# A one-core encoder block: sum reads and held squares in the gates, paced splits and other tile homes in the first MLP product, weight sums and pre-sums on other engines in the second

## The chip, the cores and the metric

The kernel runs on one core of a Trainium2 chip. The time is the device time of one execution in microseconds (us), given as the median of several runs; lower is better. The core has five engines that run side by side, each through its own list of instructions in order, and wait for each other by semaphores: TensorE (PE in the profile; its weight loads are PEld), VectorE (DVE), ScalarE (ACT), GpSimd (POOL) and SyncE (SP), which here issues the transfers (DMA).

## The reference, cut to what matters

One layer of an encoder with 1024 tokens of width 1024, all in float32:

```python
u = rms_norm(x, norm1_g)
q, k, v, cb, cc, ch, ga, gb = split(u @ w_in)
y_a = neighbourhood_attention(rms_norm(q), rms_norm(k), v, rpb) @ w_attn_branch
y_b = short_gated_conv(cb, cc, ch, conv_w) @ w_conv_branch
x = x + (sigmoid(ga) * y_a + sigmoid(gb) * y_b) @ w_o
x = x + square(relu(rms_norm(x, norm2_g) @ w_mlp_in)) @ w_mlp_out      # 1024 -> 4096 -> 1024
```

The change touches three stages: the gates (`ga`, `gb` with the products of the branches), the first MLP product (`w_mlp_in`) and the second (`w_mlp_out`).

## The kernel before, in words

**Arithmetic.** Every float32 operand is scaled by a power of two and split into two float16 halves, a head (the rounded value, made by ScalarE) and a rest (what is left, made by VectorE as scale x value - head). A product is three passes of matmuls: head x head, head x rest, rest x head. The scale comes from a bound on the operand: a sum of squares (ScalarE), added over the partitions by a matmul with ones, and turned into a power of two by five tiny VectorE instructions. Gates and both MLP products use seven products of half-size blocks in place of eight (sums and differences of blocks of weights and activations ahead, sums of products after); in the chunks 6 to 13 of the first MLP product one of the seven is cut in seven once more ("deep").

**Order of the work.** It is written out by hand. `unit` (L207) issues one group of usually 12 matmuls of 512 columns, then one turn of each hook, then the `post` of the unit before it (the VectorE or ScalarE instructions that read its PSUM bank), and then some turns of the two lists of generators: `step` for the foreground list `fg` (what must follow a product: relu, square, sums, store) and `tick` for the background list `bg` (what prepares weights to come). A turn of `bg` advances its first generator only; if that one answers `WAIT` and `side` is set, the next one gets the turn. So the two last arguments of `unit` set how early, in each engine's list, the preparation is issued. `apart` (L182) makes a generator wait until a number of units, or of matmul columns (`work`), has been issued. `need` and `built` run the background until an operand is complete. PSUM has eight banks, in three tags, taken in a fixed rota.

**Scale of an operand.** `scale_of` (L1152) waits for n units after the column of sums is ready, issues the matmul with ones (`all_sum`, L200), lets one more unit pass (`lag=1`), and only then issues VectorE's read of the result (L204) and the power of two (L435 to L442). `parts` (L1187) then issues heads (L1197) and rests (L1193) of three or four pieces, one turn each, a rest one turn after its head.

**Gates** (eight blocks n): seven units for the gates and four for the branches per block. While block n runs, `prep_s(n+1)` (L1211) scales the rows, sums blocks of weights on GpSimd (L1182), and makes the operand `w_s`. `norms1` (L1285) are three hooks that load each of 28 pieces of the first MLP weights into spare room and square them on ScalarE (L1296), a load and four units later a square; they are started after the gate units of block 2.

**First MLP product** (16 chunks q). `main1` (L1524) makes the operand of chunk q: GpSimd sums blocks (L1520), ScalarE and VectorE split, into the tile with tag V (even q) or B (odd q), not before chunk q-2 has been issued. `quad` (L1803) runs a whole chunk for q = 0 to 5, 14 and 15 (`whole`), with 2 background turns a unit for 2 < q < 14 and 5 otherwise; `pair` runs the deep chunks 6 to 13, whose extra operand `w_d` lies in the tile with tag K. After each chunk `h_done` (L1775) does relu (L1780) and square (L1782) on ScalarE, the block sums on GpSimd (L1408, VectorE for q = 0 and 1), and stores the result (L1794) to DRAM. SP takes all transfers in the order in which they are issued.

**Second MLP product** (four chunks s of seven pairs o; pair n = 7s + o). `prep2` (L1984) squares the weights (L1999, L2002), sums them, makes the pre-summed block T2 on GpSimd (L2008, L2009), and then for each pair loads the stored activation (`h_load`, L1980), splits it (L2034, L2036) and the weights (L2039, L2045) into a tile `ops` whose home rotates over the tags K, V and B, and updates blocks of weights for later pairs by GpSimd sums (L2050, L2054, L2058). Each pair is four units of 12 matmuls; their posts add into `acc` (L2135) or into the output `x` (L2144). In the last chunk `combine` (L2101) adds the accumulators into the output, partly on VectorE (L2108, L2112, L2115), partly on GpSimd (L2106, L2110, L2114), and each block of the output is stored as it is complete.

## Time and profile before

| | |
|---|---|
| median of 3 runs (range) | 1205.78 us (1203.58 to 1205.84) |
| the profiled execution: time, span | 1205.79 us, 1204.0 us |
| granted TensorE clock | 0.999 |
| gates / output product / first MLP product / second, by the trace | from about 298 / 530 / 614 / 904 us to 1199 us |

The span is the time from the first to the last instruction of the trace; the profiled execution took 1.8 us more than its span. Rows of the view of waits read: engine, the tile written and its line, the engine, tile and line waited for, and then the microseconds in total, how often, and the longest. Rows in order of time read: start, duration, engine, line, operation, tile written <- tiles read, shape, number of instructions merged, and in brackets the idle time before and what ended it. Rows of groups read: line, engine, operation, tiles, shape, count | busy us, mean ns of one | idle before. L12 is line 12 of the kernel; SPq is SP's queue of transfers. A matmul's end is modelled, so a matmul is drawn past the start of the next one.

### The profile page before, as it was taken

What the parts mean: (1) busy time and instruction counts of PE and PEld (TensorE: products, weight loads), DVE (VectorE), ACT (ScalarE), POOL (GpSimd) and SP (SyncE); (2) the same over time, 40 slices, a digit from 0 to 9 for tenths busy, and PEclk for the clock granted to TensorE, in tenths of its full rate; (3) what the DMA queues carried; (4) which work ended last, traced back from release to release, by engine and by line L of the source; (5) the groups of instructions that cost most, each with busy time, mean ns of one, the idle gap of its engine ahead of it and who ended that gap; (6) DMA issues with size and microseconds to landing.
All of it is one profiled execution on the core that took longest, in us unless ns stands there. A gap on an engine that the chain in (4) does not pass through costs nothing.

```text
span 1204.0 us, 16986 instructions
## 1 busy us (share of the span) xinstructions
PE 1186.2 (99%) x6265; PEld 579.7 (48%) x6265; DVE 975.0 (81%) x1654; ACT 754.7 (63%) x1175; POOL 455.3 (38%) x292
## 2 busy tenths in 40 slices
PE   8999999999999999999999999999998999999998
PEld 6444445555444444444477445555443444444443
DVE  6799888897468687878877767777559899999997
ACT  7866578776655767537766576667576743636440
POOL 2630011223221212001021567787677471554562
PEclk9999999999999999999999999999999999999999
DMA  9949456676544454442474445445465926335302
GB/s 289 216 160 206 109 127 137 115 147 135 114 114 139 159 183 149 140 166 114 97 165 143 156 158 192 176 142 181 158 236 201 369 80 226 121 138 194 105 35 105
DMA packets 181283, 189.61 MB, mean 157 GB/s; under 512 B 138192, under 2 KB 138704, under 8 KB 177104
## 3 DMA queue, kind: packets, MB, share of 16 engines
q1 hardware_dynamic: 181200, 188.52, 51.9%
q8 instruction: 49, 0.80, 0.3%
q14 instruction: 34, 0.28, 0.1%
HBM read 117.19 MB, written 37.75 MB: 129 GB/s over the span
## 4 chain that ended last, share of the span: by engine, by line
PE 61%; DVE 23%; ACT 8%; issue 5%; DMA 2%; SPq 0%; DVEq 0%; POOL 0%; ACTq 0%
PE ps_s L210 19%; PE ps_d L210 18%; PE ps_o L210 13%; PE ps_d L1069 8%; DVE ops L2045 2%; DVE ops L2036 2%; DVE w_s L1193 2%; PE ps_s L989 1%; PE ps_o L1046 1%; DVE w L1193 1%; DVE s L507 1%; ACT as L1782 1%; DMA w2x<-in_weights 1%; DVE sg L1342 1%; DVE w_ws L300 1%
## 5 line engine op out<-in xcount | busy, mean ns | idle before, releaser
L210 PEld LDWEIGHTS <-ops 128*128 128x128 f16 x1356 | 132.3, 98 | 162.0 <-issue 5.2
L210 PEld LDWEIGHTS <-w 128*128 128x128 f16 x1272 | 124.3, 98 | 129.3 <-DVE w L1193 1.6
L1069 PE MATMUL ps_d<-uT,w_ws 128*128 128x512 f16 x528 | 123.7, 379 | 0.0
L1408 POOL TENSOR_TENSOR as<-as 128x512 f32<-128x512 f32 x56 | 104.1, 1858 | 47.4 <-ACT as L1782 44.1
L210 PE MATMUL ps_d<-ops 128*128 128x512 f16 x516 | 118.4, 379 | 0.7 <-DVE ops L2045 0.7
L210 PE MATMUL ps_s<-ops 128*128 128x512 f16 x492 | 113.2, 379 | 2.6 <-DVE ops L2045 2.6
L2034 ACT ACTIVATE ops<-hf,sc 128x2048 f16<-128x2048 f32 x26 | 52.0, 2000 | 90.3 <-PE ps_s L210 47.1
L210 PEld LDWEIGHTS <-w_s 128*128 128x128 f16 x588 | 56.7, 98 | 70.6 <-DVE w_s L1193 2.9
L1520 POOL TENSOR_TENSOR tsum<-raw 128x512 f32<-128x512 f32 x28 | 39.4, 1417 | 126.9 <-ACT raw L1511 126.9
L210 PEld LDWEIGHTS <-uT 128*128 128x128 f16 x528 | 51.4, 98 | 62.1 <-issue 0.2
L210 PE MATMUL ps_o<-ops 128*128 128x512 f16 (+1 forms) x348 | 77.1, 372 | 0.7 <-DVE x L2144 0.7
L1069 PEld LDWEIGHTS <-w_ws 128*128 128x128 f16 x528 | 51.3, 98 | 54.1
L2036 DVE SCALAR_TENSOR_TENSOR ops<-hf,sc,ops 128x2048 f16<-128x2048 f32 x26 | 74.0, 2847 | 2.3 <-ACT ops L2034 2.2
L1182 POOL TENSOR_TENSOR gsum<-raw 128x512 f32<-128x512 f32 x14 | 19.1, 1377 | 134.5 <-ACT raw L1168 115.0
L210 PE MATMUL ps_d<-u2T,w 128*128 128x512 f16 (+1 forms) x288 | 60.9, 361 | 0.9 <-DVE as L1824 0.9
L1193 DVE SCALAR_TENSOR_TENSOR w<-raw,sc,w 128x1024 f16<-128x1024 f32 (+1 forms) x20 | 24.2, 1220 | 44.0 <-ACT w L1197 44.0
L1780 ACT ACTIVATE as<-as 128x2048 f32<-128x2048 f32 (+1 forms) x18 | 30.9, 1718 | 42.3 <-DVE as L1857 25.7
L1193 DVE SCALAR_TENSOR_TENSOR w<-tsum,sc,w 128x1024 f16<-128x1024 f32 x28 | 50.7, 1834 | 5.1 <-ACT w L1197 5.1
L210 PE MATMUL ps_s<-u2T,w 128*128 128x512 f16 (+1 forms) x252 | 52.7, 359 | 0.0
L1012 ACT ACTIVATE sz<-sz,sc 128x384 f32<-128x384 f32 (+1 forms) x64 | 37.2, 582 | 23.9 <-DVE sc L1003 16.6
L309 ACT ACTIVATE w_ws<-raw,sc 128x512 f16<-128x512 f32 (+2 forms) x72 | 40.6, 637 | 17.8 <-DVE sc L282 17.8
L210 PE MATMUL ps_s<-u2x,w 128*128 128x512 f16 (+1 forms) x228 | 49.8, 368 | 0.0
(419 smaller groups left out, 2720.0 us busy)
## 6 DMA issues: line engine op xcount, KB each, us to landing
raw<-in_weights SPq DMA_DIRECT2D x97, 512.0 KB, 4.5
hs<-as SPq DMA_DIRECT2D x16, 1792.0 KB, 7.9
hf<-hs SPq DMA_DIRECT2D x26, 1024.0 KB, 6.3
w2x<-in_weights SPq DMA_DIRECT2D x16, 512.0 KB, 7.4
raw<-in_weights SPq DMA_DIRECT2D x16, 384.0 KB, 3.5
mL<-in_weights SPq DMA_DIRECT2D x10, 512.0 KB, 4.5
mH<-in_weights SPq DMA_DIRECT2D x9, 512.0 KB, 4.3
xt<-in_x SPq DMA_DIRECT2D x8, 512.0 KB, 8.2
```

What stands on the lines that cost most here:

```text
L210: T.matmul(ps, l, r, start=a, stop=b, skip_group_check=free)
L309: A.activation(self.parts[:, 0, f + o:f + o + m], self.raw[p][:, o:o + m], AF.Copy, scale=sc[:, c:c + 1])
L1012: A.activation(z, z, AF.Exp, scale=-1.0, bias=sc[:, d["mx"]], accum_out=sc[:, d["sm"]])
L1069: T.matmul(ps, l, r, start=a, stop=b)
L1182: G.tensor_tensor(t[:, o], a, b, op=OP.add)
L1193: V.scalar_tensor_tensor(o(1), w, sc[:, s], o(0), op0=OP.mult, op1=OP.subtract)
L1408: sub.tensor_tensor(z[o], z[a], z[b], op=op)
L1520: G.tensor_tensor(t[:, o], a, b, op=OP.add)
L1780: A.activation(v[:, 0:4], v[:, 0:4], AF.Relu)
L2034: A.activation(P[:, 1, 0], hf, AF.Copy, scale=sc[:, Rs])
L2036: V.scalar_tensor_tensor(P[:, 1, 1], hf, sc[:, Rs], P[:, 1, 0], op0=OP.mult, op1=OP.subtract)
L2045: V.scalar_tensor_tensor(P[:, 0, 1, sl], w[i2], sc[:, fw], P[:, 0, 0, sl], op0=OP.mult, op1=OP.subtract)
```

## The change

- Gates: `prep_s` reads the sum at the first turn after its matmul (`lag` 0 in place of 1). From there until the operand is split, the hooks get no turns (`hold`). The hooks start after the gate units of block 1 in place of 2.
- First MLP product: for chunks 4 and 5 the rests are issued at most one per unit (`pace`). Chunks 3 to 5 give 4 background turns a unit in place of 2. The operand of chunk 15 may be made once chunk 12 has been issued (before: chunk 13), and goes into the tile with tag V; chunk 14's goes into the one with tag K. The homes of the `ops` tiles are shifted by one accordingly (pair 0 in B, 1 in K, 2 in V, and so on).
- Second MLP product: for s = 0 the scale waits three units in place of four. The weight sums after w11 and t2 are VectorE's (L2050, L2054); the one after t3 stays on GpSimd.
- Last chunk: the pre-sums of the accumulators (a6 with a1, a7 with a6) pass from VectorE to GpSimd, and are made one product earlier: a1 is added into a6 before the last product of a6 is added there, and a6 into a7 likewise.

```diff
@@ -176,7 +176,7 @@
-    late, units, forced, side, hooks = [], [0], [False], [False], []
+    late, units, forced, side, hooks, hold = [], [0], [False], [False], [], [False]
     work = [0]
@@ -209,7 +209,7 @@
         for g in list(hooks):
-            if not advance(g):
+            if not hold[0] and not advance(g):
                 hooks.remove(g)
@@ -1149,12 +1149,12 @@
-    def scale_of(am, more, n=3):
+    def scale_of(am, more, n=3, lag=1):
...
         b, s, inv = cols_of("prep", 1), cols_of("prep", 1), keep()
-        yield from all_sum(a, b, anybank(), 1e-36)
+        yield from all_sum(a, b, anybank(), 1e-36, lag)
         yield from pow2_half(b, 14, s, inv, more)
@@ -1184,12 +1184,17 @@
-    def parts(todo, s, then):
+    last_low = [-9]
+
+    def parts(todo, s, then, pace=False):
...
                 o, w = prev
+                if pace:
+                    yield from apart(last_low[0], 1)
+                    last_low[0] = units[0]
                 V.scalar_tensor_tensor(o(1), w, sc[:, s], o(0), op0=OP.mult, op1=OP.subtract)
@@ -1214,12 +1219,14 @@
         yield from forms_sum(ch, t, 2)
-        s, ch.inv = yield from scale_of(ch.sum, 9, 2)
+        s, ch.inv = yield from scale_of(ch.sum, 9, 2, 0)
+        hold[0] = True
         while done[0] < ch.first:
...
         ch.split = True
+        hold[0] = False
@@ -1328,7 +1335,7 @@
             sg = gate_units(n)
-            if n == 2:
+            if n == 1:
                 rooms = [v[:, 6:8].rearrange("p a t -> p (a t)").bitcast(F32) for v in M]
@@ -1343,6 +1350,7 @@
             branch_units(n, post)
+            assert n < 6 or not hooks
             late.append(lambda n=n, mf=mf: fg.append(m_done(n, mf)))
@@ -1464,7 +1472,7 @@
     pe_done, ready = [-2], set()
-    TAGS = ((base2, "B"), (base, "K"), (base, "V"))
+    TAGS = {i: ((base2, "B"), (base, "K"), (base, "V"))[(i - 16) % 3] for i in range(16, 44)}
     tsum = {}
@@ -1527,12 +1535,13 @@
             yield from sums_main(q)
-        while pe_done[0] < q - 1:
+        while (pe_done[0] < 1 if q == 2 else pe_done[0] < min(q - 1, 13)) or q == 14 and sub_done[0] < 12:
             yield
         m = int(deep)
-        pool, tag = ((base, "V"), (base2, "B"))[q % 2]
+        pool, tag = {14: (base, "K"), 15: (base, "V")}.get(q) or ((base, "V"), (base2, "B"))[q % 2]
         P = pool.tile([128, 7 - m, 2, 512], F16, name="w16_1", tag=tag)
         P1[q] = lambda w, i, k: P[:, w - m, i, k * 128:k * 128 + 128]
+        pace = q in (4, 5)
         todo = [] if deep else [(0, 1, ch.r[0][:, 0:1])]
@@ -1541,7 +1550,7 @@
         yield from parts([((lambda i, a=a, b=b: P[:, a - m:b - m, i]), w) for a, b, w in todo],
-                         at(s1, q // 2 - 1), then)
+                         at(s1, q // 2 - 1), then, pace)
         ready.add(q)
@@ -1557,7 +1566,7 @@
                           ((0, 2, x[:, 0].rearrange("p (h c) -> p h c", h=2)), (2, 3, y[:, 0:1, 256:]), (3, 7, d))],
-                         at(s1, q // 2 - 1), lambda n: None)
+                         at(s1, q // 2 - 1), lambda n: None, False)
         ready.add((0, q))
@@ -1835,7 +1844,7 @@
             2: lambda ps: V.tensor_tensor(z[0], ps[2], z[4], op=OP.add),
-            7: post7, 3: post3}, 2 if c1 == 512 else 3, 2 if 2 < q < 14 else 5, (1, 2, 5, 4, 6, 7, 3) if c0 else (1, 6, 5, 4, 2, 7, 3))
+            7: post7, 3: post3}, 2 if c1 == 512 else 3, 4 if 2 < q < 14 else 5, (1, 2, 5, 4, 6, 7, 3) if c0 else (1, 6, 5, 4, 2, 7, 3))
@@ -1991,7 +2000,7 @@
             yield from gate(16)
-            OPS[16] = TAGS[16 % 3][0].tile([128, 2, 2, 2048], F16, name="ops", tag=TAGS[16 % 3][1])
+            OPS[16] = TAGS[16][0].tile([128, 2, 2, 2048], F16, name="ops", tag=TAGS[16][1])
             j = OPS[16][:, 0, 0].bitcast(BF16)
@@ -2010,10 +2019,10 @@
             yield from gate(17)
-            P = OPS[17] = TAGS[17 % 3][0].tile([128, 2, 2, 2048], F16, name="ops", tag=TAGS[17 % 3][1])
+            P = OPS[17] = TAGS[17][0].tile([128, 2, 2, 2048], F16, name="ops", tag=TAGS[17][1])
             later["h", 1] = P[:, 0].rearrange("p w m -> p (w m)").bitcast(F32).rearrange("p (k t) -> p k t", k=4)
             SP.dma_start(later["h", 1], HS[0][:, ORDER[1][0]])
-        sw, inv = yield from scale_of(sums, 0, 4)
+        sw, inv = yield from scale_of(sums, 0, 3 + (s > 0))
         fw = keep()
@@ -2022,7 +2031,7 @@
             yield from gate(i)
-            pool, tag = TAGS[i % 3]
+            pool, tag = TAGS[i]
             if n > 1:
@@ -2047,11 +2056,11 @@
                 for i2 in range(2):
-                    G.tensor_tensor(w11[i2], w11[i2], w12[i2], op=OP.add)
+                    V.tensor_tensor(w11[i2], w11[i2], w12[i2], op=OP.add)
                 yield
...
                 for i2 in range(2):
-                    G.tensor_tensor(w12[i2], w12[i2], w22[i2], op=OP.add)
+                    V.tensor_tensor(w12[i2], w12[i2], w22[i2], op=OP.add)
                 yield
@@ -2104,13 +2113,11 @@
             G.tensor_tensor(x11, x11, a1, op=OP.add)
+            G.tensor_tensor(a6, a6, a1, op=OP.add)
         elif o == 1:
-            V.tensor_tensor(a6, a6, a1, op=OP.add)
-            yield
             G.tensor_tensor(x12, x12, a6, op=OP.subtract)
+            G.tensor_tensor(a7, a7, a6, op=OP.add)
         else:
-            V.tensor_tensor(a7, a7, a6, op=OP.add)
-            yield
             G.tensor_tensor(x22, x22, a7, op=OP.subtract)
```

## The prediction, as it was put on record

> **What bounds the kernel now.** I read the totals first, then which engines the matmul engine waited for, then TensorE in order of time around each wait.
>
> ```profile
> span 1204.0 us, 16986 instructions
> PE 1186.2 (99%) x6265; PEld 579.7 (48%) x6265; DVE 975.0 (81%) x1654; ACT 754.7 (63%) x1175; POOL 455.3 (38%) x292
> ```
> ```profile
> PE ps_s L210 <- DVE ops L2045: 2.6, 2, 1.8
> PE ps_s L210 <- DVE w_s L1193: 1.1, 1, 1.1
> PE ps_d L210 <- DVE w L1193: 1.1, 1, 1.1
> PE ps_d L210 <- DVE as L1824: 0.9, 1, 0.9
> ...
> PE ps_o L210 <- DVE x L2144: 0.7, 1, 0.7
> PE ps_d L210 <- DVE ops L2045: 0.7, 1, 0.7
> ...
> PE ps_d L210 <- DVE w_s L1193: 0.2, 1, 0.2
> ```
> ```profile
> 910.29 2.75 PE L210 MATMUL ps_o<-ops 128*128 128x512 f16 x12
> 912.88 2.75 PE L210 MATMUL ps_d<-ops 128*128 128x512 f16 x12
> 915.48 0.38 PE L210 MATMUL ps_s<-ops 128*128 128x512 f16 x1
> ...
> 920.97 2.75 PE L210 MATMUL ps_d<-ops 128*128 128x512 f16 x12
> ```
>
> TensorE is busy all the time; no engine beside it bounds a stage for long. An undisturbed unit of twelve matmuls begins 2.59 us after the last (910.29 to 912.88), and the change neither adds nor drops a matmul. So the time can fall only by the stops of TensorE, and rise only by new ones. The stops that the edited code touches sum to 0.2+1.1 (gates), 1.1+0.9 (first MLP product), 0.7+2.6 and 0.7 (second product, and its last chunk): 7.3 us in eight stops. Each costs more than it shows, because a matmul's end is drawn past the start of the next: the unit at 915.48 lasts 5.49 us, 2.90 over the normal 2.59, while its two pieces in the waits are 2.6 together. So about 0.16 a stop, and 7.3 + 8 x 0.16 = **8.6 us** is all there is to win, 0.7% of the time. All eight wait for VectorE; the question is what makes VectorE late at each.
>
> **Gates: sum read sooner, squares held (cost of the stops 1.3 + 2 x 0.16 = 1.6).** The stop of 1.1, at 448 us, in order of time on TensorE, VectorE and ScalarE:
>
> ```profile
> 436.09 0.17 PE L201 MATMUL ps_o<-ones 128*128 128x1 bf16 x1
> ```
> ```profile
> 439.16 0.75 DVE L1342 SCALAR_TENSOR_TENSOR sg<-ps_s,sc,sg 128x512 f32<-128x512 f32 x1 [2.07 <-ACT sg L1275]
> 439.82 0.15 DVE L204 TENSOR_SCALAR sc<-ps_o 128x1 f32<-128x1 f32 x1
> ...
> 445.68 2.47 DVE L1193 SCALAR_TENSOR_TENSOR w_s<-gsum,sc,w_s 128x1024 f16<-128x1024 f32 x2
> ```
> ```profile
> 437.12 2.00 ACT L1275 ACTIVATE sg<-sg,sc 128x2048 f32<-128x2048 f32 x1 [1.97 <-DVE sg L1273]
> ...
> 441.29 1.76 ACT L1197 ACTIVATE w_s<-raw,sc 128x512 f16<-128x512 f32 x2 [1.13 <-DVE sc L441]
> ...
> 444.00 1.04 ACT L1296 ACTIVATE mL<-mL 128x1024 f32<-128x1024 f32 x1
> ```
>
> The sum is there at 436.26 and is read at 439.82, behind the posts of the next unit. With lag 0 the read stands ahead of them, in the 2.07 us in which VectorE waits for the sigmoid; the heads (L1197) then start when the sigmoid ends, 439.1, not 441.29: 2.2 us sooner, against a stop of 1.3. The read is an added wait on TensorE's sum; what queues behind it on VectorE is the next post, which needs the same unit's end anyway. It could cost up to a unit (2.59) for each of seven groups if VectorE had other work there; the idle 2.07 says it has not, so I take the gain. Holding the squares back takes 1.04 from between the heads, already within the 2.2: no further gain. They start a block earlier instead, 28 of them with their loads of 512 KB: on a ScalarE busy 63% its idle time is the cover, and without it each would cost its 1.04; for the loads an issue holds SP about 0.5 (the row of 905.52 below), three in five units, with no TensorE wait on a load in this stage. **-1.6.**
>
> **First MLP product: splits paced, four turns a unit (stops 1.1+0.9+0.32 = 2.3).**
>
> ```profile
> 677.85 0.60 ACT L1835 ACTIVATE as<-ps_d 128x512 f32<-128x512 f32 x1 [4.24 <-DMA hs<-as]
> ...
> 682.28 1.75 ACT L1197 ACTIVATE w<-raw,sc 128x512 f16<-128x512 f32 x2
> ```
> ```profile
> 678.48 0.69 DVE L1816 TENSOR_TENSOR as<-ps_s,as 128x512 f32<-128x512 f32 x1 [2.47 <-ACT as L1835]
> 683.02 3.47 DVE L1193 SCALAR_TENSOR_TENSOR w<-raw,sc,w 128x512 f16<-128x512 f32 x2 [3.85 <-ACT w L1197]
> ...
> 687.01 3.91 DVE L1193 SCALAR_TENSOR_TENSOR w<-tsum,sc,w 128x1024 f16<-128x1024 f32 x2
> ```
>
> Chunk 4's heads stand behind L1835, the relu and the square, and VectorE idles 2.47+3.85. With four turns a unit instead of two, the first head is issued ahead of L1835 (into its 4.24 us of waiting), the second between relu and square; the rests (L1193) follow one a unit. The last rest then ends near 689.1 instead of 690.92, and TensorE needs it at 689.5: the 1.1 stop goes, by a margin of 0.4. Pacing by itself works against this: it puts the last rest one unit later in VectorE's program. The second stop (L1824) is VectorE's lag behind TensorE by a whole chunk; posts come about 1.75 us sooner, TensorE 1.26 sooner, so 0.5 at most is won; I take 0.3 of 1.06. Ends: 0 and 2.3. **-1.5.** The new homes: chunk 15 no longer waits for chunk 13's tile, which matters next.
>
> **Second product, start (0.7+2.6+0.48 = 3.8).** The queue of loads, ScalarE, VectorE:
>
> ```profile
> 872.31 4.26 SPq L237 DMA_DIRECT2D raw<-in_weights  x2
> ...
> 905.52 0.52 SPq L1794 DMA_DIRECT2D hs<-as  x1
> 906.14 4.29 SPq L1980 DMA_DIRECT2D hf<-hs  x4
> ```
> ```profile
> 884.16 2.00 ACT L2002 ACTIVATE ops<-w2x,sc 128x2048 bf16<-128x2048 f32 x1 [2.18 <-DMA w2x<-in_weights]
> ...
> 916.72 2.00 ACT L2034 ACTIVATE ops<-hf,sc 128x2048 f16<-128x2048 f32 x1 [3.50 <-DMA hf<-hs]
> ```
> ```profile
> 889.61 0.16 DVE L1148 TENSOR_REDUCE sc<-sc 128x1 f32<-128x6 f32 x1 [7.93 <-ACT ops L2002]
> ...
> 913.97 5.87 DVE L2045 SCALAR_TENSOR_TENSOR ops<-h,sc,ops 128x1024 f16<-128x1024 f32 x2
> ```
>
> VectorE stands still for 7.93 us, with chunk 14's posts behind it, for squares that wait for w2x, which sits in SP's queue behind two raw loads that wait for chunk 15's rests. Chunk 15 is now split while chunk 13 runs, so the raw loads go at about 868 instead of 872 to 876 and w2x 7 us sooner; ScalarE then reaches the squares at about 875 and the sum comes at about 884.6, not 889.6: **5 us sooner for everything behind it**, the store of 905.52 and the four hf loads queued behind it too. The sum's matmul moves up one more unit (three units' wait, not four). Against this, VectorE gets two adds of 1024 before and two after the operands at 913.97. Of the work of the second pair the end moves from 919.8 to about 913.4; TensorE, 0.83 sooner there, needs it by 915.9 (915.48 - 0.83, and half a unit for the second half of the operand). What is late next: pair 2, whose head waits for hf (916.72); it moves with the store to about 912, and its last rest to 924.6, against a need of 926.3. All three stops go: **-3.8**; ends 0 and 3.8.
>
> **Adds traded between engines (0.7+0.16 = 0.9).** Groups from 921 us on:
>
> ```profile
> L2045 DVE SCALAR_TENSOR_TENSOR ops<-t,sc,ops 128x1024 f16<-128x1024 f32 x12 | 27.4, 2324 | 0.0
> L2135 DVE SCALAR_TENSOR_TENSOR acc<-ps_s,sc,acc 128x512 f32<-128x512 f32 x15 | 11.1, 739 | 0.0
> ...
> L2054 POOL TENSOR_TENSOR raw<-raw,w2x 128x1024 f32<-128x1024 f32 x6 | 19.9, 3331 | 0.0
> ...
> L2106 POOL TENSOR_TENSOR x<-x,acc 128x512 f32<-128x512 f32 x4 | 8.0, 2028 | 5.3 <-DVE acc L2135 5.3
> ...
> L2108 DVE TENSOR_TENSOR acc<-acc,acc 128x512 f32<-128x512 f32 x4 | 6.1, 1524 | 0.1
> L2112 DVE TENSOR_TENSOR acc<-acc,acc 128x512 f32<-128x512 f32 x4 | 3.6, 909 | 0.1
> L2045 DVE SCALAR_TENSOR_TENSOR ops<-h,sc,ops 128x1024 f16<-128x1024 f32 x2 | 2.5, 1273 | 0.0
> ```
>
> A VectorE pass over 1024 takes 1.27 alone (L2045 from h) and 2.32 on average where GpSimd runs (from t). The four weight sums of a chunk cost VectorE an estimated 4 x 1.27 = 5.1 and free it of four GpSimd adds, each of which stretched a pass by about 1 to 2 us: 4 to 8 back. I take the sum as nothing; ends -3 and +5 a chunk, with VectorE's slack between. In the last chunk, eight pre-sums leave VectorE: 6.1 + 3.6 = 9.7 us, and pass to GpSimd, where they must end before the post (L2135) that reads them; posts read PSUM and take 0.74 also beside GpSimd. At L2106's mean of 2.03, GpSimd's last pre-sum ends near 1176, when VectorE would want it. VectorE then reaches L2144 about 2 to 3 us sooner, and the stop of 0.7 before the last group goes: **-0.9**.
>
> The Trainium skill's page SBUF — State Buffer, section Who interferes with whom, says that a VectorE instruction with two SBUF inputs and a GpSimd one that reads SBUF lock each other out for a whole instruction. By that rule each pre-sum could wait out a pass of 2.3 us, and the last rival below would hold. The trace agrees in part: L2135, with one PSUM input, keeps 739 ns, L2045 does not keep its 1273.
>
> **Sum.** 1205.79 (the profiled execution; 1.8 outside its span of 1204.0, and 0.01 from the median of the three runs) - 1.6 - 1.5 - 3.8 - 0.9 = **1198.0**.
>
> **Rivals.**
> 1. The wait moves on in the second product. If w2x does not come sooner (loads share the memory, and chunk 12's store goes out just then), only the unit of the sum (2.59) is won, the adds take it back, and pair 2 still waits for hf: 3 of the 3.8 come back. 1201. For: hf stands behind a store behind GpSimd. Against: SP's order shows nothing else that holds w2x.
> 2. Pacing moves the first product's stop: the last rest waits for a post that is late, and the stop grows from 1.26 to a unit, 2.6, with the second stop unchanged: 1198.0 + 1.5 + 1.3 = 1201. Against: VectorE idles 6 us just before.
> 3. The change doesn't do what it says: what now hides behind each VectorE wait is as late, all but the gates' 1.6 comes back: 1204.2.
> 4. Slower: GpSimd becomes the end of the last chunk. It has 4 + 4 sums and pre-sums for output one, two adds of 1024, and 4 + 4 more, all ahead of VectorE's last posts. At 3.33 each (L2054, the dear end) 16 x 3.33 + 2 x 3.33 = 60 us from 1139 ends at 1199, 23 after the 1176 above, some 17 after VectorE's slack: 1198 + 17 = 1215. It makes the whole slower from a mean of about 2.7 us on; L2106 has 2.03.
>
> **Chances.** Forecast 0.60 (its own range 1196 to 1199.8); rivals 1 and 2 together 0.23; rival 3 0.07; rival 4 0.10. The range takes in the forecast and rivals 1 and 2, with room for the runs' own spread: 1195.5 to 1203.2; it leaves out 0.17. About 0.2% (2.4 us) is what a measurement of this kernel can tell from no change: faster needs under 1203.4, so 0.83 (forecast, 1 and 2); same 0.07 (rival 3); slower 0.10 (rival 4).
>
> **What would show it.** Gates: no TensorE wait on w_s, L204 at once behind the sum's matmul. First product: the wait on w gone, that on L1824 about 0.7. Second: VectorE's 7.93 at L1148 down to about 3, w2x issued before 872, no wait on ops. End: L2106 and its pre-sums done before 1176 in today's times. A new TensorE wait above 1 us anywhere, or VectorE waiting for GpSimd in the last chunk, makes the prediction wrong.

## The result and the profile after

| | before | after |
|---|---|---|
| median (range), 6 runs each | 1204.82 us (1203.41 to 1207.51) | 1198.30 us (1197.27 to 1199.86) |
| ratio, 95% interval | | 0.9946 [0.9932, 0.9960] |
| profiled execution: time, span | 1205.79 us, 1204.0 us | 1198.30 us, 1196.2 us |

The changed kernel is faster by 0.54%, and 1198.3 stands against a forecast of 1198.0. The sum was right within 0.3, and partly by luck: 7.8 of stops were forecast and 6.97 won, 0.8 of the last store filled the gap, and the forecast started from the profiled execution, 0.97 above the median of the six runs (by the medians the gain is 6.5). Several of its steps were not right. First the totals of the changed kernel and what TensorE waited for. The lines of the code have moved by 5 to 9 (the add of chunk posts L1824 is L1833, the rest L1193 is L1198, the weights' rest L2045 is L2054).

```profile
span 1196.2 us, 16986 instructions
PE 1185.5 (99%) x6265; PEld 580.4 (49%) x6265; DVE 955.2 (80%) x1662; ACT 755.5 (63%) x1175; POOL 410.8 (34%) x284
```
```profile
PE ps_o L210 <- DVE as L1866: 1.2, 1, 1.2
...
PE ps_d L210 <- DMA uT<-gs: 0.4, 1, 0.4
```

All the waits of before that the edited code touched are gone. Two others stand in their place, 1.2 on a post of the first product's chunk 7 (L1866) and 0.4 on a transposing transfer in the gates. A stop costs about 0.16 more than the wait shows, as the prediction has it; the costs below are from matmul start to matmul start, less the matmul's own 0.21 us (0.11 for those of 256 columns). Before there are nine, not the eight that the prediction counts: the 0.2 that its view shows for w_s is two stops, of 0.38 and 0.28.

| cost of TensorE's stops, us | gates | first product | second, start | end | sum |
|---|---|---|---|---|---|
| before | 0.38 + 0.28 + 1.31 | 1.24 + 1.06 | 0.83 + 0.91 + 2.00 | 0.85 | 8.86 |
| after | 0.57 | 1.32 | 0 | 0 | 1.89 |
| gained | 1.40 | 0.98 | 3.74 | 0.85 | 6.97 |
| forecast | 1.6 | 1.5 | 3.8 | 0.9 | 7.8 |

The profiled execution fell by 7.49: these 6.97; 0.8 because the last store took 0.8 less behind VectorE's last instruction (3.07 us instead of 3.87, nothing that the change does), and 0.3 back that lies outside the span.

**Gates.** All engines of the changed kernel in order of time, at the place that the prediction shows:

```profile
438.52 0.17 PE L201 MATMUL ps_d<-ones 128*128 128x1 bf16 x1
...
438.75 0.16 DVE L204 TENSOR_SCALAR sc<-ps_d 128x1 f32<-128x1 f32 x1 [1.39 <-PE ps_d L201]
...
440.23 1.76 ACT L1202 ACTIVATE w_s<-raw,sc 128x512 f16<-128x512 f32 x2 [2.61 <-DVE sc L441]
...
441.90 2.17 ACT L1202 ACTIVATE w_s<-gsum,sc 128x1024 f16<-128x1024 f32 x2
...
444.24 2.47 DVE L1198 SCALAR_TENSOR_TENSOR w_s<-gsum,sc,w_s 128x1024 f16<-128x1024 f32 x2
```

The read (L204) follows the sum's matmul by 0.23 us instead of 3.73. But that matmul now comes a unit later, 438.52 for 436.09, and VectorE waits 1.39 for it; the heads start 1.06 sooner, not 2.2. The two heads of gsum stand side by side with no square between them, and the last rest ends at 446.71 instead of 448.15.

**First product.** The same, at chunk 4's operand, and then at the new stop:

```profile
676.87 0.69 DVE L1825 TENSOR_TENSOR as<-ps_s,as 128x512 f32<-128x512 f32 x1 [1.38 <-ACT as L1844]
...
682.73 3.57 DVE L1198 SCALAR_TENSOR_TENSOR w<-tsum,sc,w 128x1024 f16<-128x1024 f32 x2 [1.14 <-ACT w L1202]
...
688.74 0.68 DVE L1838 TENSOR_TENSOR as<-ps_s,as 128x512 f32<-128x512 f32 x1
...
688.82 0.53 SPq L1803 DMA_DIRECT2D hs<-as  x1
```
```profile
753.45 1.36 DVE L1198 SCALAR_TENSOR_TENSOR w<-raw,sc,w 128x1024 f16<-128x1024 f32 x1 [4.54 <-ACT w L1202]
...
754.73 2.29 DVE L1198 SCALAR_TENSOR_TENSOR w<-tsum,sc,w 128x1024 f16<-128x1024 f32 x1
...
757.54 1.69 DVE L1198 SCALAR_TENSOR_TENSOR w<-tsum,sc,w 128x1024 f16<-128x1024 f32 x1
...
759.76 0.68 DVE L1866 TENSOR_TENSOR as<-ps_o,as 128x512 f32<-128x512 f32 x1
...
760.48 1.89 PE L210 MATMUL ps_o<-u2T,w 128*128 128x512 f16 x8 [1.16 <-DVE as L1866]
```

Chunk 4's rests end at 686.30 (before 690.92), the posts of chunk 3 behind them at 689.42 (before 694.04). At 759 VectorE stands idle 4.54 us for ScalarE's head, then has the rests and posts in a row, just as before (there 4.55). It comes 1.36 sooner than before, but TensorE comes 3.8 sooner, by the gates and the two stops of this product, and now has to wait for it.

Earlier on VectorE had gained as much as TensorE: its post of L1838 runs at 724.55, 3.9 sooner than before (728.43). It lost most of that here, beside GpSimd's work ahead of it:

```profile
716.16 3.48 POOL L1416 TENSOR_TENSOR as<-as 128x512 f32<-128x512 f32 x2 [4.66 <-ACT as L1791]
...
719.60 3.48 POOL L1528 TENSOR_TENSOR tsum<-raw 128x512 f32<-128x512 f32 x2
...
725.62 2.62 POOL L1416 TENSOR_TENSOR as<-as 128x512 f32<-128x512 f32 x2
...
737.70 0.42 DVE L1866 TENSOR_TENSOR as<-ps_s,zt 128x256 f32<-128x256 f32 x1 [2.86 <-DMA hs<-as]
```

VectorE, and ScalarE for 5.40 at 737.68, wait for the store of chunk 4, which was issued at 728.27; before it was issued at 727.10, and ScalarE waited 0.25 for it. The store follows chunk 4's four block sums (L1416) on GpSimd. Before they stand in a row; here four weight sums (L1528) stand between them, since more of a split's turns are issued in a unit. So the four turns also brought forward what GpSimd does for the split, and a later chunk's tile comes free late by it. This is read from the rows; no run moves these sums alone.

**Second product.** SP's queue, the squares and VectorE:

```profile
871.22 2.26 SPq L237 DMA_DIRECT2D w2x<-in_weights  x4
...
879.46 2.00 ACT L2011 ACTIVATE ops<-w2x,sc 128x2048 bf16<-128x2048 f32 x1
...
883.72 0.16 DVE L1148 TENSOR_REDUCE sc<-sc 128x1 f32<-128x6 f32 x1 [7.72 <-ACT ops L2011]
...
887.10 0.15 DVE L204 TENSOR_SCALAR sc<-ps_s 128x1 f32<-128x1 f32 x1
...
903.31 2.34 DVE L2045 SCALAR_TENSOR_TENSOR ops<-ops,sc 128x2048 f16<-128x2048 f32 x1
...
908.69 2.47 DVE L2054 SCALAR_TENSOR_TENSOR ops<-h,sc,ops 128x1024 f16<-128x1024 f32 x2
```

The sum is there at 883.72 instead of 889.61; the wait in front of it is still 7.72, since VectorE's work ahead of it moved up as well. ScalarE goes straight from the squares of raw to those of w2x (L2011), where before it waited 2.18 and 1.23 for the loads. Pair 1's operand ends at 911.16, 8.7 us sooner, 1.1 ahead of TensorE (912.23).

**End.** What VectorE waited for from 1120 us on, and the last chunk's adds:

```profile
DVE acc L2142 <- POOL acc L2116: 2.8, 2, 1.7
```
```profile
L2054 DVE SCALAR_TENSOR_TENSOR ops<-t,sc,ops 128x1024 f16<-128x1024 f32 x12 | 16.9, 1447 | 0.0
...
L2119 POOL TENSOR_TENSOR acc<-acc,acc 128x512 f32<-128x512 f32 x4 | 10.6, 2649 | 0.0
...
L2116 POOL TENSOR_TENSOR acc<-acc,acc 128x512 f32<-128x512 f32 x4 | 6.1, 1513 | 0.0
```

VectorE does wait for GpSimd's pre-sums, 2.8 us in all, and no stop of TensorE comes of it. VectorE's pass from t fell from 2324 to 1447 ns on average, since fewer GpSimd adds run beside it.

### The profile page after: what moved, and what is told of

Same layout as the page of the kernel before. It is cut to its first block, busy times and chain, and to the rows that moved or that the text cites. A ratio compares the mean times of both kernels' runs of the same rounds, so it can differ in the third digit from the quotient of the medians.

```text
span 1196.2 us, 16986 instructions
## 1 busy us (share of the span) xinstructions
PE 1185.5 (99%) x6265; PEld 580.4 (49%) x6265; DVE 955.2 (80%) x1662; ACT 755.5 (63%) x1175; POOL 410.8 (34%) x284
## 4 chain that ended last, share of the span: by engine, by line
PE 61%; SPq 4%; issue 3%; POOL 3%; DVE 2%; DMA 2%; ACT 2%; DVEq 0%; POOLq 0%; ACTq 0%
PE ps_s L210 23%; PE ps_d L210 23%; PE ps_o L210 16%; SPq L1140 3%; POOL tsum L1528 2%; DMA hs<-as 1%; POOL as L1416 1%; DVE w L1198 1%; ACT raw L1519 1%; DVE tsum L1562 0%; DVE as L1866 0%; ACT as L1789 0%; ACT as L1791 0%; DMA uT<-gs 0%; ACT w L1202 0%
## 5 line engine op out<-in xcount | busy, mean ns | idle before, releaser
L210 PEld LDWEIGHTS <-ops 128*128 128x128 f16 x1356 | 132.5, 98 | 157.3
L210 PEld LDWEIGHTS <-w 128*128 128x128 f16 x1272 | 124.4, 98 | 128.2 <-issue 1.3
L1416 POOL TENSOR_TENSOR as<-as 128x512 f32<-128x512 f32 x56 | 99.3, 1773 | 58.3 <-ACT as L1791 55.1
L210 PE MATMUL ps_d<-ops 128*128 128x512 f16 x516 | 118.2, 379 | 0.0
L210 PE MATMUL ps_s<-ops 128*128 128x512 f16 x492 | 112.9, 379 | 0.0
L2043 ACT ACTIVATE ops<-hf,sc 128x2048 f16<-128x2048 f32 x26 | 52.0, 2000 | 85.9 <-PE ps_d L210 26.9
L210 PEld LDWEIGHTS <-w_s 128*128 128x128 f16 x588 | 56.8, 98 | 69.1 <-issue 0.9
L1528 POOL TENSOR_TENSOR tsum<-raw 128x512 f32<-128x512 f32 x28 | 40.6, 1462 | 129.6 <-ACT raw L1519 129.6
L210 PEld LDWEIGHTS <-uT 128*128 128x128 f16 x528 | 51.4, 98 | 62.1
L210 PE MATMUL ps_o<-ops 128*128 128x512 f16 (+1 forms) x348 | 77.1, 372 | 0.0
L2045 DVE SCALAR_TENSOR_TENSOR ops<-hf,sc,ops 128x2048 f16<-128x2048 f32 x26 | 67.6, 2601 | 3.5 <-ACT ops L2043 3.5
L210 PE MATMUL ps_d<-u2T,w 128*128 128x512 f16 (+1 forms) x288 | 61.0, 361 | 0.0
L1198 DVE SCALAR_TENSOR_TENSOR w<-tsum,sc,w 128x1024 f16<-128x1024 f32 x28 | 49.0, 1771 | 9.3 <-ACT w L1202 9.3
L1182 POOL TENSOR_TENSOR gsum<-raw 128x512 f32<-128x512 f32 x14 | 19.1, 1375 | 106.2 <-ACT raw L1168 63.7
L1198 DVE SCALAR_TENSOR_TENSOR w<-raw,sc,w 128x1024 f16<-128x1024 f32 (+1 forms) x20 | 24.1, 1216 | 38.4 <-ACT w L1202 38.4
L210 PE MATMUL ps_s<-u2T,w 128*128 128x512 f16 (+1 forms) x252 | 52.7, 359 | 0.0
L300 DVE SCALAR_TENSOR_TENSOR w_ws<-raw,sc,w_ws 128x512 f16<-128x512 f32 (+2 forms) x72 | 43.8, 667 | 6.0 <-ACT w_ws L309 6.0
```

The source lines that it names most:

```text
L210: T.matmul(ps, l, r, start=a, stop=b, skip_group_check=free)
L300: V.scalar_tensor_tensor(lo, self.raw[p][:, o:o + m], sc[:, c:c + 1], hi, op0=OP.mult, op1=OP.subtract)
L1198: V.scalar_tensor_tensor(o(1), w, sc[:, s], o(0), op0=OP.mult, op1=OP.subtract)
L1416: sub.tensor_tensor(z[o], z[a], z[b], op=op)
L1528: G.tensor_tensor(t[:, o], a, b, op=OP.add)
L2043: A.activation(P[:, 1, 0], hf, AF.Copy, scale=sc[:, Rs])
```

## The experiments

Twelve kernels, each the changed kernel with one or several parts taken back or moved, and one profiled execution of each. Times are medians (range) beside runs of the kernel before on the same chip. Since a median carries more than the edit (TensorE's first matmul at L210 starts between 22.3 and 25.4 us in these profiles, in code that is the same in all), the verdicts go by the profile: **TensorE's run**, from the start of that matmul to the start of the last one, as a difference from the changed kernel's (1169.34 us), and the costs of its stops. The one on the transposing transfer (after 339 us, in the gates' column in brackets) was between 0 and 1.05 in kernels that don't differ there, and the one at 759 between 0.93 and 1.68, so differences in the run below about 1 us are not read.

| kernel | time, us | ratio to before | run | gates | first | second, start | end |
|---|---|---|---|---|---|---|---|
| changed | 1198.30 (1197.27 to 1199.86) | 0.9946 [0.9932, 0.9960] | 0 | (0.57) | 1.32 | 0 | 0 |
| e1 | 1200.64 (1199.21 to 1200.99) | 0.9971 [0.9961, 0.9980] | +1.15 | 1.96 | 1.14 | 0 | 0 |
| e2 | 1199.91 (1198.82 to 1204.58) | 0.9973 [0.9963, 0.9982] | +4.1 | 1.26 (0.89) | 2.22 | 0 | 0 |
| e3 | 1202.07 (1201.28 to 1204.70) | 0.9989 [0.9981, 0.9998] | +3.5 | (1.05) | 4.39 | 0 | 0 |
| e4 | 1202.31 (1200.82 to 1204.35) | 0.9987 [0.9978, 0.9996] | +4.0 | (0.32) | 4.08 | 0 | 0 |
| e5 | 1199.05 (1198.42 to 1200.68) | 0.9964 [0.9950, 0.9978] | +0.8 | (1.04) | 1.01 | 0.52 | 0 |
| e6 | 1198.02 (1196.98 to 1198.97) | 0.9952 [0.9939, 0.9965] | -0.9 | 0 | 0.93 | 0 | 0 |
| e7 | 1199.09 (1198.24 to 1201.08) | 0.9963 [0.9950, 0.9976] | +1.0 | (0.52) | 1.23 | 0 | 1.10 |
| e8 | 1197.33 (1196.80 to 1198.95) | 0.9950 [0.9937, 0.9963] | -0.4 | (0.47) | 1.04 | 0 | 0 |
| e9 | 1201.19 (1200.37 to 1203.60) | 0.9978 [0.9969, 0.9987] | +3.3 | (0.42) | 1.68 | 2.01 | 1.11 |
| e10 | 1201.63 (1200.23 to 1202.54) | 0.9981 [0.9973, 0.9990] | +2.5 | 0 | 1.47 | 1.74 | 1.11 |
| e11 | 1198.58 (1197.10 to 1199.34) | 0.9954 [0.9941, 0.9966] | +0.2 | (0.79) | 1.22 | 0 | 0 |
| e12 | 1197.45 (1197.10 to 1198.26) | 0.9947 [0.9934, 0.9959] | -0.5 | (0.42) | 1.05 | 0 | 0 |

### e1: the gates as before

```diff
-        s, ch.inv = yield from scale_of(ch.sum, 9, 2, 0)
-        hold[0] = True
+        s, ch.inv = yield from scale_of(ch.sum, 9, 2)
-            if n == 1:
+            if n == 2:
```

> The changed kernel with the gates as before (sum read a unit later, squares not held, hooks from block 2). The gates' stops of TensorE before were 0.38, 0.28 and 1.31 us (at 331.8, 389.3, 446.7); the changed kernel has one of 0.57 at 339.3 that waits for a transfer. Theory (the gates gained the difference, 1.4 us, because the stop at 331.8 had only covered the transfer's lateness): the three stops return, that at 339.3 goes, time 1199.7. Rival (the transfer is late because the squares' loads start a block earlier): the three return and add 1.97, and the stop at 339.3 is then worth 0.57 of its own, which shows when the hooks alone are put back.

The three stops came back with the costs of before (0.38, 0.27, 1.31), and that on the transfer went; the run is 1.15 longer. The theory fits: the transfer was as late before, under the stop at 331.8. That the stop on it went is weak evidence by itself, since it is 0 in e6 and e10 too, which keep the new gates. The time's ratio shows more, 0.0025 of it or 3 us, between intervals that nearly touch; the profile shows nothing for the rest.

### e2: the early read alone

```diff
-        hold[0] = True
-            if n == 1:
+            if n == 2:
```

> The changed kernel without the hold and with the hooks from block 2; the sum is still read at the first turn. Theory (the earlier read alone makes the heads early enough, holding the squares adds nothing): no stop of TensorE at 389 and 446, stop at 339.3 as in the changed kernel (0.57, a chain of transfers on SP), time within 0.3 us of 1198.3. Rival A (the squares between the heads matter): a stop of 0.5 to 1.3 comes back near 446. Rival B (the early hooks delay the transfer): the stop at 339.3 goes, 1197.7.

The stops at 389 and 446 stay away, so the early read is what removes them. Two others came, at places where nothing stood before or after. Of this kernel, the waits, and then ScalarE and VectorE before the first of them:

```profile
PE ps_s L201 <- DVE ones L331: 0.7, 1, 0.7
...
PE ps_o L201 <- DVE ones L331: 0.2, 1, 0.2
```
```profile
408.08 1.04 ACT L1302 ACTIVATE raw<-raw 128x1024 f32<-128x1024 f32 x1
...
409.12 1.99 ACT L1281 ACTIVATE sg<-sg,sc 128x2048 f32<-128x2048 f32 x1
411.01 2.17 ACT L1202 ACTIVATE w_s<-gsum,sc 128x1024 f16<-128x1024 f32 x2
```
```profile
412.18 2.48 DVE L1198 SCALAR_TENSOR_TENSOR w_s<-gsum,sc,w_s 128x1024 f16<-128x1024 f32 x2 [2.47 <-ACT w_s L1202]
...
418.45 0.16 DVE L331 CAST ones<-sc 128x1 bf16<-128x1 f32 x1
```

A square (L1302) slips in front of the sigmoid (L1281); the heads start 1.08 later than in the changed kernel (409.93), of which 0.53 is this kernel's being later there as a whole, and so come the rests and, behind them on VectorE, the column of another sum (L331). In the changed kernel that column is ready 0.24 before TensorE wants it; here TensorE stands before the sum's matmul, 0.38 at 418 us. The second stop, 0.88 at 476, has another cause: there the heads are no later than the whole kernel is (0.89). An add of four columns ahead of the column (L102, 474.98) takes 1.21 instead of 0.17, beside a GpSimd add of 1.27 (L1182, 474.90). In the changed kernel that GpSimd add comes at 472.98, ahead of it; here three squares instead of two stand ahead of the scaling that it waits for (L1168, 473.13 for 471.21). This run takes back the hold and the earlier hooks together, so these 1.26 us are what the two are worth, not the hold alone; neither theory nor rival A named the places. Rival B falls: the transfer is as late with the late hooks. The profiled execution took 1202.96, 3 us above its kernel's median: its stop at 761 us is 2.22 where the others have 0.9 to 1.7, and the clock fell behind it, as told at the end; so about 2.5 of its 4.1 are not the edit's.

### e3 and e4: pacing and turns, one without the other

```diff
-        pace = q in (4, 5)
+        pace = False
```

> The changed kernel with the rests of chunks 4 and 5 not paced, four turns a unit kept. Theory (the turns do the work, pacing works against it): no stop at 689 nor at 726, the stop at 759 unchanged at 1.3, time within 0.3 us of 1198.3. Rival (pacing keeps the posts from queueing behind rests): a stop on a post (the add after the first products) of 0.5 to 1.1 comes back near 726, and 1198.8 to 1199.4.

```diff
-            ... 4 if 2 < q < 14 else 5, ...
+            ... 2 if 2 < q < 14 else 5, ...
```

> The changed kernel with two background turns a unit in chunks 3 to 5 as before, pacing kept. Theory: the stops before, 1.24 at 689 and 1.06 at 726, return, and the stop of 1.32 at 759 goes since it is the same lateness met later: net +1.0, 1199.3. By the prediction's second rival pacing with two turns puts the last rest a unit later: the stop at 689 grows to 2.6 or more, 1200.6. If the turns did nothing: 1198.3 with the stop at 759.

Both theories fell. Each half alone costs more than the kernel before has here: 3.22 us of stops at 714 to 728 without pacing, 4.08 at 689 and 725 with two turns, against 2.30. (TensorE comes 1.4 sooner here than before, by the gates; no run has neither half with the new gates.) Without pacing (all times of that execution are 3.3 later here, 2.8 of it from the start on):

```profile
684.88 3.49 POOL L1416 TENSOR_TENSOR as<-as 128x512 f32<-128x512 f32 x2 [3.75 <-ACT as L1791]
...
688.56 3.26 POOL L1528 TENSOR_TENSOR tsum<-raw 128x512 f32<-128x512 f32 x2 [0.19 <-ACT raw L1519]
...
689.37 0.68 DVE L1825 TENSOR_TENSOR as<-ps_s,as 128x512 f32<-128x512 f32 x1
...
694.36 2.62 POOL L1416 TENSOR_TENSOR as<-as 128x512 f32<-128x512 f32 x2
...
697.00 0.53 SPq L1803 DMA_DIRECT2D hs<-as  x1
...
705.31 0.60 ACT L1844 ACTIVATE as<-ps_o 128x512 f32<-128x512 f32 x1 [3.69 <-DMA hs<-as]
```

With four turns a unit all rests are issued ahead of the chunk's first post (L1825, in the kernel before L1816), which then waits behind VectorE's idle 4.20: it runs at 689.37, in the changed kernel at 676.87. The chain that ends at TensorE is another one, on GpSimd. The square ahead of chunk 2's block sums (L1416) is no later in this kernel's own time (682.72 less 3.3, for 679.58), but the split's four weight sums (L1528) stand between these block sums; in the changed kernel the four block sums stand in a row (681.74, 7.05 us) and the weight sums follow at 688.75. So chunk 2's store goes out some 5 us late in this kernel's own time (697.00 for 688.82, less 3.3); ScalarE waits 3.69 for it before it can copy chunk 4's first product into the tile, and TensorE then stands at chunk 4's posts. Pacing here puts the first post into VectorE's idle time and GpSimd's weight sums behind the block sums. With two turns and pacing, the lateness comes at chunk 6's operand:

```profile
716.69 1.99 ACT L1791 ACTIVATE as<-as,sc 128x2048 f32<-128x2048 f32 x1
...
719.15 1.13 ACT L1202 ACTIVATE w<-raw,sc 128x1024 f16<-128x1024 f32 x1
...
720.32 1.48 DVE L1198 SCALAR_TENSOR_TENSOR w<-raw,sc,w 128x1024 f16<-128x1024 f32 x1 [7.08 <-ACT w L1202]
...
728.07 4.10 PE L210 MATMUL ps_d<-u2T,w 128*128 128x512 f16 x11 [2.87 <-DVE as L1833]
```

The head (L1202) stands behind the square, where the changed kernel has it between relu and square (712.96); VectorE idles 7.08 with seven posts behind the rest. That the stop at 759 goes when TensorE stops earlier was right.

### e5 to e7: the start of the second product, one part at a time

```diff
-        while (pe_done[0] < 1 if q == 2 else pe_done[0] < min(q - 1, 13)) or q == 14 and sub_done[0] < 12:
+        while pe_done[0] < q - 1:
-        pool, tag = {14: (base, "K"), 15: (base, "V")}.get(q) or ((base, "V"), (base2, "B"))[q % 2]
+        pool, tag = ((base, "V"), (base2, "B"))[q % 2]
-    TAGS = {i: (...)[(i - 16) % 3] for i in range(16, 44)}
+    TAGS = {i: (...)[i % 3] for i in range(16, 44)}
```

> The changed kernel with the homes of chunks 14, 15 and of the operands as before, so that chunk 15 is split only after chunk 13. Theory (the earlier split lets the loads and the squares go sooner, and that is the second product's gain): the column of sums comes at about 887 to 889 instead of 883.7, TensorE's stops at the second product's first pairs return; 3.7 us were there before, the unit less of waiting for the sum takes up to 2.6 off: 1.1 to 3.7, so 1199.4 to 1202, nearest 1201.5. Rival (the shorter wait for the sum was enough): no stop, 1198.3.

One stop of 0.52, at pair 2, under the lower end that the theory gave. The sum comes at 885.13, 1.4 later than in the changed kernel, not 3 to 5 us: w2x is issued 2.8 later here, but ScalarE waits only 0.84 and 0.39 for it.

```diff
-        sw, inv = yield from scale_of(sums, 0, 3 + (s > 0))
+        sw, inv = yield from scale_of(sums, 0, 4)
```

> The changed kernel with the scale of the second product's first weights read after four units, not three. The operands of the first pairs are done 1.3 and 1.1 us ahead of TensorE in the changed kernel. Theory (the homes bring 5 us, the shorter wait one unit, 2.59): the margins fall by up to 2.6 to -1.3 and -1.5, half a unit of which the second half of an operand may be late, so stops of 0 to 1.5 together, 1198.3 to 1199.8, nearest 1198.8. Rival (VectorE reaches the read late anyway): no stop, 1198.3.

Nothing: the sum is read at 891.07 instead of 887.10, and pair 1's operand still ends 1.5 ahead. ScalarE needs the scale only after the head of the activation (L2043, 890.33 here), which waits for nothing that the sum gives.

```diff
-                    V.tensor_tensor(w11[i2], w11[i2], w12[i2], op=OP.add)
+                    G.tensor_tensor(w11[i2], w11[i2], w12[i2], op=OP.add)
...
-                    V.tensor_tensor(w12[i2], w12[i2], w22[i2], op=OP.add)
+                    G.tensor_tensor(w12[i2], w12[i2], w22[i2], op=OP.add)
```

> The changed kernel with the weight sums after w11 and t2 back on GpSimd; the pre-sums stay there too. Theory (the trade is even as long as there is slack; the pre-sums on GpSimd cured the end): VectorE's passes from t and w2x go back from 1.45 and 1.91 to about 2.3 and 2.4 us, no new stop over 0.5 in the middle, pair 2's operand is the one at risk: 1198.3 to 1199. The last rival of the prediction (GpSimd ends the last chunk): four more sums of 3.3 to 3.9 us, some 14 us, move its last pre-sum from 1169.5 to as late as 1183, and VectorE wants it at 1182: a stop of 1 to 3 us near the end, 1199 to 1201.

No stop at the start, though pair 1's operand ends 1.57 after TensorE reaches it (its second half is not needed at once), and a stop of 1.10 at the end, where the pre-sums still are GpSimd's. GpSimd's last pre-sum ends at 1171.0, at most 1.5 later than in the changed kernel (1169.5), and VectorE's last wait for it is over by then: the last rival's mechanism isn't this stop.

### e8: the pre-sums back on VectorE

```diff
-            G.tensor_tensor(a6, a6, a1, op=OP.add)
         elif o == 1:
+            V.tensor_tensor(a6, a6, a1, op=OP.add)
+            yield
             G.tensor_tensor(x12, x12, a6, op=OP.subtract)
-            G.tensor_tensor(a7, a7, a6, op=OP.add)
         else:
+            V.tensor_tensor(a7, a7, a6, op=OP.add)
+            yield
             G.tensor_tensor(x22, x22, a7, op=OP.subtract)
```

> The changed kernel with the last chunk's pre-sums back on VectorE, in their old places; weight sums stay VectorE's. Theory (the pre-sums made VectorE late at the end): VectorE gets 9.7 us of adds back, and the stop of 0.85 before the last group returns or grows, 1199.2 or up to 1201. Rival (the weight sums moved to VectorE freed it of GpSimd's interference and that cured the end): no stop, 1198.3.

No stop. With e7 that settles the end: the weight sums on VectorE cure it, the pre-sums on GpSimd do not. The last two weight rests of e7 show why, beside those of before:

```profile
1176.44 4.49 DVE L2054 SCALAR_TENSOR_TENSOR ops<-w2x,sc,ops 128x1024 f16<-128x1024 f32 x2
```
```profile
1184.73 2.47 DVE L2045 SCALAR_TENSOR_TENSOR ops<-w2x,sc,ops 128x1024 f16<-128x1024 f32 x2
```

With the pre-sums on GpSimd its last adds (L2121, 1170.97 to 1179.84 in e7) lie beside VectorE's last two rests, which take 4.49 for 2.47, and L2122 takes 0.98 four times for 0.69. That is 3.2 back of the 3.6 (L2112, four adds) that VectorE was freed of there. On balance they bring VectorE nothing: its last weights' rest ends 2.24 ahead of TensorE's next group in the changed kernel and 2.51 ahead in e8, 0.27 less with the pre-sums on GpSimd. What the weight sums give is there before the pre-sums begin: VectorE's rests of w2x start 0.84 ahead of TensorE's group (the 300th matmul from the end) in the changed kernel and in e8, 1.07 behind it before and 1.06 in e7: 1.9 us from the weight sums.

### e9 and e10: the start of the second product, parts together

e9 is e5, e6 and e7 in one; e10 leaves the scale at three units:

```diff
-        while (pe_done[0] < 1 if q == 2 else pe_done[0] < min(q - 1, 13)) or q == 14 and sub_done[0] < 12:
+        while pe_done[0] < q - 1:
...
-                    V.tensor_tensor(w11[i2], w11[i2], w12[i2], op=OP.add)
+                    G.tensor_tensor(w11[i2], w11[i2], w12[i2], op=OP.add)
...
```

> The changed kernel with the whole start of the second product as before: homes of chunks 14, 15 and operands, four units for the scale, weight sums on GpSimd (pre-sums stay on GpSimd). Undone one at a time these gave stops of 0.52 (homes), 0 and 0 at the start. Theory A (they cover for each other, each worth something and the slack hides it): in the changed kernel pair 1's second operand ends 1.1 us ahead; homes took 1.3 of that, weight sums 2.6; together it ends about 2.9 late, of which some 1.4 is free (e7 had 1.57 without a stop), so a stop of about 1.5 at pair 1, with 1.1 at the end as with weight sums on GpSimd: 2.6 over the changed kernel. Theory B (the prediction's): the three are the gain of the second start, 3.7 of stops at 900 to 918 return, with the 1.1 at the end 4.8 over it. Rival C (the start came right only because the stages before came 2.4 us earlier): no stop at the start, only the 1.1.

> The changed kernel with the homes as before and the weight sums on GpSimd, the scale still after three units. Theory A: as with all three undone, within 0.3 us (the shorter wait for the sum does nothing, since ScalarE is busy until the head of the activation either way): a stop of about 1.5 at pair 1. Rival: the shorter wait saves the rest of the unit, 2.59, once the others are old: no stop at the start.

Theory A holds: 2.01 and 1.74 at pair 1, where one at a time they gave 0.52, 0 and 0; the scale's unit is worth nothing in either setting. e9's VectorE and GpSimd at pair 1, against the rows of 903.31 and 908.69 above:

```profile
902.43 7.70 POOL L2059 TENSOR_TENSOR raw<-raw 128x1024 f32<-128x1024 f32 x2
...
903.48 4.43 DVE L2045 SCALAR_TENSOR_TENSOR ops<-ops,sc 128x2048 f16<-128x2048 f32 x1
...
910.09 5.66 POOL L2063 TENSOR_TENSOR raw<-raw,w2x 128x1024 f32<-128x1024 f32 x2
910.94 5.88 DVE L2054 SCALAR_TENSOR_TENSOR ops<-h,sc,ops 128x1024 f16<-128x1024 f32 x2
```

Beside GpSimd's adds these three passes take 10.3 us. In the changed kernel they take 4.8, behind an add (L2059, two instructions) of 2.35: 3.1 sooner for the pair. The homes bring 1.4 more. Before, the stops were 3.74, not 2.01. Most of the rest, 1.4, is in the landing of w2x: the second of its squares ended 12.9 us after the first issue before (876.63 to 889.49), 11.5 in e9, with the same queue ahead of it. Why the loads took 1.4 longer in that one profile isn't settled.

### e11 and e12: the new stop in the first product

```diff
-            main(n, ps, i, post, 1 if i == 3 and n < 15 else more)
+            main(n, ps, i, post, 1 if i == 3 and n < 15 else 0 if n == 7 and i in (5, 2) else more)
```

> The changed kernel, and in chunk 7's units 5 and 2 no background turns, so that two adds of VectorE on chunk 7's first products stand ahead of chunk 8's first rests and not between them; nothing else moves on any engine. Theory (the stop of 1.32 at 759 is VectorE's: it idles 4.5 us for ScalarE's head with those adds queued behind the rests): the adds fall into the idle time, the add that frees the bank ends 1.3 to 1.5 us sooner, and the stop goes or falls under 0.3: 1.3 below the changed kernel. Rival (the head is what holds it, the order does not matter): the stop stays at 1.0 to 1.3. Second rival (the stop moves on to the next chunk's bank): 0.5 to 1.0 elsewhere before 800.

> The same order in chunk 7 and the last chunk's pre-sums back on VectorE, as before. With the pre-sums alone undone there was no stop at the end. Theory: no stop at 759 and none at the end, all stops together under 1.5 (those at 137, 256 and 339 that the change does not touch), equal to the former within 0.3; the pre-sums on GpSimd are worth nothing. Rival (the pre-sums matter once TensorE comes earlier): a stop of 0.3 to 0.9 at the end.

The two posts moved into the idle time as meant (one to 750.08), and the stop at 759 fell to 0.72; but 0.50 came up at 767:

```profile
753.90 1.36 DVE L1198 SCALAR_TENSOR_TENSOR w<-raw,sc,w 128x1024 f16<-128x1024 f32 x1 [3.13 <-ACT w L1202]
755.18 4.50 DVE L1198 SCALAR_TENSOR_TENSOR w<-tsum,sc,w 128x1024 f16<-128x1024 f32 x2
...
765.22 1.72 DVE L1198 SCALAR_TENSOR_TENSOR w<-raw,sc,w 128x1024 f16<-128x1024 f32 x1 [2.69 <-ACT w L1202]
```

The last two rests take 4.50 beside GpSimd's block sums where they took 2.29 + 1.69, and the next operand's head is as late as ever. The second rival holds in part: the stop moved on to the next operand, but 0.72 of it stayed, and both stops together (1.22) lie within what kernels with the old order have at 759 alone (0.93 to 1.68). So the posts' order is not the bound of these chunks; the lateness of ScalarE's heads, which e11 leaves alone, is the likelier one, and behind it the store told above. e12 keeps a stop at 759 too (0.55, and 0.50 at 767), against its theory, and has none at the end, as e8; its time (ratio 0.9947) is that of the changed kernel. No version here is clearly faster.

## Why the prediction was right, and where it was not

- **Frame: right.** Only TensorE's stops could be won, and the time fell by them: 6.97 of 8.86. The forecast kept 0.76 of an old stop; that one went, and 1.89 of new ones came at other places.
- **Gates, -1.6 forecast, 1.40 measured.** The early read is what removes the stops (e2). "No further gain" from holding the squares is the step that failed: with the earlier hooks it is worth 1.26 (e2), 0.38 by ScalarE's order and 0.88 by an add of VectorE's beside one of GpSimd's; against that the transfer's stop takes 0 to 1.05. The heads' gain of 2.2 was mis-sized, 1.06, as the sum's matmul is issued a unit later. The wait added to VectorE (1.39) was harmless, as argued.
- **First product, -1.5 forecast, 0.98 measured.** "Pacing by itself works against this" failed: without it the four turns cost 3.22 (e3), and the last rest ends no sooner (689.4 less 3.3, for 686.30). The step costed when rests end, and not what else the turns bring forward: GpSimd's weight sums, ahead of block sums, a store and a later chunk's tile. By the rows that is also what kept VectorE late for 759. The stop on the post was forecast to keep 0.7; it went, and more than that, 1.32, came at 759.
- **Second product, -3.8 forecast, 3.74 measured.** The size was right partly by luck, the cause mostly not: the sum was forecast 5 us sooner, by the homes. Of the 5.9 us by which the sum is earlier the homes bring 1.4; 2.4 came from the stages before, and about 2 from loads of w2x that landed sooner after their issue. The weight sums, taken as nothing, are the largest part, 2.6 (e7) to 3.1 (e9) for pair 1. Undone alone each is covered by the others.
- **End, -0.9 forecast, 0.85 measured.** The pre-sums were named as the cause; they give back 3.2 of the 3.6 they free there, and on balance bring VectorE nothing (2.24 ahead with them, 2.51 without). The weight sums are the cause (e7, e8).
- **Rivals.** Rivals 1 to 3 did not come: w2x is issued 5.4 sooner (871.22 for 876.63), the stop on the last rest at 689 went, and all four places gained. Rival 4 (GpSimd ends the last chunk) needed a mean above 2.7 us; its eight pre-sums have 2.08 (L2116 1.51, L2119 2.65). The Trainium skill's page SBUF — State Buffer, section Who interferes with whom, by which two-input passes and GpSimd's reads lock each other out, agrees with the pair in e9 (2.94 us a pass beside GpSimd, 1.24 without), and it is VectorE's rests that paid, not the posts.
- **Signs.** "L1148's wait down to about 3" and "VectorE waiting for GpSimd makes it wrong" were poor signs: the wait stayed 7.72 with the sum 5.9 sooner, and 2.8 us of waits for GpSimd cost nothing. A new TensorE wait above 1 us came too, the 1.2 at 759, and the forecast still held.

## What to carry to other kernels

Where stops are small and many, undo parts in pairs as well as singly: here three parts read 0.5, 0 and 0 alone and 2.0 together, and two others each cost time alone and won it together. Cost an instruction that is moved ahead by what then stands behind it on its engine, up to the next tile that has to come free, and not by its own end; and look at every engine that the same list of work feeds, here GpSimd's sums beside VectorE's rests. Moving adds between VectorE and GpSimd has a second price, the stretch of whatever runs beside them; read it from the same pass with and without the neighbour.

## What the runs showed of the hardware

The two longest stops of TensorE were followed by a lower clock. In e4 a stop of 3.03 at 725 us, and in e2 one of 2.22 at 761, were followed by seven matmuls of 0.43 us in place of 0.21, 1.5 to 1.7 us more each time. The granted clock (PEclk, the first number after POOL's) over those stretches, of e4 and of e2:

```profile
728.10:731.00 2.90, 2.90 (x7) 0.99 (x7) 2.17 (x4) 1.03 (x1) 2.90 (x3) 0.50 0.39 152
```
```profile
764.40:767.40 3.00, 3.00 (x9) 1.03 (x8) 1.03 (x3) 2.27 (x2) 2.92 (x3) 0.50 1.05 411
```

The clock is halved for at least these 2.9 and 3.0 us, at once behind the stop in e4 and 1.2 us after it in e2. Stops of 2.00 (before) and 2.01 (e9) were followed by no such stretch. The Trainium skill's page TensorE: Matmul & The Clock Gate, section What's actually happening, has the clock fall to half after an idle window of about 3.4 us; here stops of 3.03 and 2.22 us were each enough once.
